# The gated delta rule on raw keys and queries, its triangular inverse from gathered left halves

## The chip, the cores and the metric

The kernel runs on one core of one Trainium2 chip. The metric is the device time of that core in microseconds (us), the median of the timed runs. Profiles come from one profiled execution, whose own time stands beside its span below.

## What is computed

Two blocks of two layers each run over 256 tokens of width 1024. The first block holds attention, a gated linear recurrence and memory attention. The second is a mixer (gated delta rule, retention, pooling, three gated branches) and a feed-forward part. The change lies in the gated delta rule alone, which runs twice, once in each layer of the second block. Cut to what matters, with 4 heads, head width 128 and chunks of 64 tokens:

```
q = l2_normalize(q); k = l2_normalize(k)          # x * rsqrt(sum(x*x) + 1e-6), per token and head
# gated_delta_rule(q, k, v, beta, g), everything per chunk of 64
q = q * dk**-0.5
G = cumsum(g); decay[i, j] = exp(G_i - G_j) for j <= i, else 0
k_beta = k * beta
m = strictly lower part of (k_beta k^T) * decay
sol = triangular_solve(m + eye, [v * beta, k_beta * exp(G)]);  u, w = sol
attn = (q k^T) * decay
q_dec = q * exp(G);  k_tail = k * exp(g_last - G)
# from chunk to chunk
v_new = u - w @ state
o = q_dec @ state + attn @ v_new
state = state * exp(g_last) + k_tail^T @ v_new
# afterwards: o * rsqrt(mean(o*o) + 1e-6) * gain
```

## The kernel before

All large products (projections, gates, branches, feed-forward) are done as three products of rounded float32 parts: a weight unit of 128x1024 is loaded into raw, ScalarE casts it to wh, VectorE takes the rest wl (class Stream), and mm3 (L537) or chan (L567) issues the products on TensorE into the PSUM tiles acc. This stream of weight products runs through the whole kernel.

Everything else is written as Python generators (tasks) that yield the tiles they wait for. While the program is being made, the class Order keeps a reckoned time of TensorE and of the other engines, with a fixed and a per-element cost for each instruction. After each few stream products poll() (L195) steps every task whose awaited tiles are reckoned ready by then (with HOP = 150 ns and SLACK = 200 ns, L151). So the program order on TensorE, which is the order in which it executes, mixes the task's small products into the stream at places that the reckoned times choose. The real engines then wait for each other by semaphores.

The delta rule is four tasks for each layer: dn_scalars (beta, g and the exponentials ex of the cumulated g), and for each tile t of 128 tokens (two chunks, 4 heads side by side) delta_tile (L1342), delta_side (L1468, spawned by it) and delta_scan (L1484). delta_tile of t = 1 starts when that of t = 0 has ended. All tiles are 128 partitions x 4 heads x 128 float32.

In delta_tile, T() transposes a tile head by head on TensorE into a PSUM tile mx, and mm() multiplies two tiles head by head into another. It transposes the convolved k and q to token rows (tiles cvk, cvq), takes their reciprocal norms (rms_heads, L432: a square on ScalarE, a sum and small steps on VectorE), makes kn and qn, transposes both back (knT, qnT), forms the decay E from psE, and M = -(beta) E * (kn kn^T) below the diagonal. kbg and ktail are kn scaled by rows.

The inverse of the unit triangular matrix is built over DN_LEVELS = (2, 4, 8, 16, 32, 64). Level 2 is a masked copy of M into W (tile dnT); its transpose is U. At each further level (the loop at L1429, n = 1 to 5) the right halves `new` of the blocks of U are replaced: a product of M with `new` into a PSUM tile, copied to X by ScalarE, a product of W with X, and a masked copy into U by VectorE; then, if n < 5, U is transposed to W for the next level. In the profile the first product reads dnU, dnM, the second dnX, dnT, and the transpose ident, dnU.

At the end the transposed v times beta and kbg are multiplied with U into u and one half of WQ. delta_side transposes the decayed query qd into the other half of WQ, and forms attnT from knT, qnT and E. delta_scan runs the recurrence over the chunks with the state st, adds the two parts of the output oi, normalises it by rms_heads and hands it on; it is transposed and used much later, in the branch "dn" behind the gates.

PSUM has 8 banks: 3 for acc, 5 for mx. SBUF tiles of these tasks come from a pool k2 of 24 buffers of 2 KB, longer ones from k4.

Of the kernel before, what the change touches and what calls it, by code (L numbers as in the profile page):

```python
# [14 lines left out]
ALU = mybir.AluOpType  # L15
# [3 lines left out]
P = 128  # L19
# [11 lines left out]
DN_LEVELS = (2, 4, 8, 16, 32, 64)  # L31
# [292 lines left out]
class Kernel:  # L324
# [15 lines left out]
    def big(self, pool, tag, shape, name, dt):  # L340
        self.uid += 1
        return pool.tile(list(shape), dt, tag=tag, name=f"{name}_{self.uid}")
# [86 lines left out]
            self.pe.transpose(tp[:, h, :], src[:, h * P : (h + 1) * P], self.ident)  # L429
        return tp  # L430

    def rms_heads(self, ps, scale=1.0 / P, eps=1e-6):  # L432

        junk = self.k2([P, 4, P], "junk")
        self.act.activation(junk, ps, AF.Square)
        yield junk
        ss = self.sm(4, "ss")
        self.dve.tensor_reduce(ss, junk, axis=AX.X, op=ALU.add)
        yield ss
        r = yield from self.rsqrt(ss, scale, eps, 4)  # L440
        return r

    def right(self, x, lev):
# [448 lines left out]
    def hgrn_z(self, lev, A, kx, qx):  # L892
# [3 lines left out]
        half = lev // 2  # L896
        E, Z = self.k2([P, 2, S], "hE"), self.k2([P, 2, S], "hZ")
        left, right = slice(0, half), slice(half, lev)
        Av, Ev, qv, kv, Zv = (x.rearrange("p h (b s) -> p (h b) s", s=lev) for x in (A, E, qx, kx, Z))
        n = 2 * S // lev  # L900
        if lev == 256:
            end = [A[:, :, 64 * c + 63 : 64 * c + 64] for c in range(3)]
            s01 = self.sm(2, "s01").unsqueeze(2)
            dve.tensor_tensor(s01, end[0], end[1], op=ALU.add)
            act.activation(E[:, :, 128:192], A[:, :, 128:192], AF.Exp)
            for c, b, scale in ((1, end[1], -1.0), (3, end[2], 1.0), (0, s01, -1.0)):
                cs = slice(64 * c, 64 * c + 64)
# [434 lines left out]
    def delta_tile(self, l, t, cv, sc, r):  # L1342

        act, dve, pe = self.act, self.dve, self.pe
        yield [f"dns{l}"] + [f"cv{l}{n}{j}" for n in "kqv" for j in range(2)] + ([f"dnt{l}0"] if t else [])
        yield [cv[n] for n in "kqv"]
        beta, g, ex = sc
        ts = slice(t * P, (t + 1) * P)
        hs = slice(4 * t, 4 * t + 4)
        bt = beta[:, t, :]  # L1350
        big = lambda tag: self.k2([P, 4, P], "dn" + tag)
        flat = lambda x: x.rearrange("p h d -> p (h d)")

        def T(c):
            tp = self.mx()
            for h in range(4):
                pe.transpose(tp[:, h, :], c[:, h, :], self.ident)
            return tp

        def mm(a, b):  # L1360
            ps = self.mx()
            for h in range(4):
                pe.matmul(ps[:, h, :], a[:, h, :], b[:, h, :], start=True, stop=True)
            return ps


        Bg = big("Bg")
        dve.tensor_tensor(Bg, self.dn_strict.unsqueeze(1).to_broadcast([P, 4, P]), self.bc(g[:, t, :]), op=ALU.mult)

        tk = T(cv["k"][:, :, ts])  # L1370
        tq = T(cv["q"][:, :, ts])
        yield [Bg, tk]
        psE = self.mx()
        for h in range(4):
            pe.matmul(psE[:, h, :], self.ident_bf, self.dn_neg, start=h == 0, stop=False, skip_group_check=True)
        pe.matmul(psE, self.dn_tri, Bg, start=False, stop=True, skip_group_check=True)
        rk = yield from self.rms_heads(tk, 1.0)
        E = big("E")
        act.activation(E, psE, AF.Exp)
        rq = yield from self.rms_heads(tq, 1.0)  # L1380
        kn = big("kn")
        dve.tensor_tensor(kn, tk, self.bc(rk), op=ALU.mult)
        yield kn
        tp = T(kn)
        bg, nb = self.sm(4, "bg"), self.sm(4, "nb")
        dve.tensor_tensor(bg, bt, ex[:, 0, hs], op=ALU.mult)
        dve.tensor_scalar(nb, bt, -1.0, None, op0=ALU.mult)
        kbg, ktail = big("kbg"), big("ktail")
        dve.tensor_tensor(kbg, kn, self.bc(bg), op=ALU.mult)
        dve.tensor_tensor(ktail, kn, self.bc(ex[:, 1, hs]), op=ALU.mult)  # L1390
        yield tp
        knT = big("knT")
        act.copy(knT, tp)

        qn = big("qn")
        dve.tensor_scalar(rq, rq, P**-0.5, None, op0=ALU.mult)
        dve.tensor_tensor(qn, tq, self.bc(rq), op=ALU.mult)

        yield knT
        psM = mm(knT, knT)  # L1400
        yield qn
        tp = T(qn)
        qd = big("qd")
        dve.tensor_tensor(qd, qn, self.bc(ex[:, 0, hs]), op=ALU.mult)
        nE = big("nE")
        dve.tensor_tensor(nE, E, self.bc(nb), op=ALU.mult)
        yield [psM, nE]
        M = big("M")
        dve.tensor_tensor(M, psM, nE, op=ALU.mult)

        W = big("T")
        mask = lambda n: self.dn_masks[:, n * P : (n + 1) * P].unsqueeze(1).to_broadcast([P, 4, P])
        act.copy(W, self.ident.unsqueeze(1).to_broadcast([P, 4, P]))
        yield [M, W]
        dve.copy_predicated(W, mask(0), M)
        yield tp
        qnT = big("qnT")
        act.copy(qnT, tp)
        yield W
        tp = T(W)  # L1420
        U = big("U")
        yield tp
        act.copy(U, tp)

        WQ = self.k4([P, 4, 2, P], "dnWQ")
        attnT = big("attnT")
        side = self.delta_side(T, mm, E, qnT, knT, qd, WQ, attnT)
        self.o.spawn(side, f"dnside{l}{t}")
        for n in range(1, 6):  # L1429
            lev = DN_LEVELS[n]  # L1430
            X = self.k2([P, 4, P // 2], "dnX")
            new = self.right(U, lev)
            yield [M, U]
            ps = self.mx((P, 4, P // 2))
            for h in range(4):
                pe.matmul(ps[:, h, :].rearrange("p (b s) -> p b s", s=lev // 2), M[:, h, :], new[:, h], start=True, stop=True)
            yield ps
            act.copy(X, ps)
            yield [X, W]
            ps = self.mx((P, 4, P // 2))  # L1440
            for h in range(4):
                pe.matmul(ps[:, h, :], W[:, h, :], X[:, h, :], start=True, stop=True)
            yield ps
            dve.copy_predicated(new, self.right(mask(n), lev), ps.rearrange("p h (b s) -> p h b s", s=lev // 2))
            if n < 5:
                yield U
                tp = T(U)
                yield tp
                W = big("T")
                act.copy(W, tp)  # L1450

        tp = T(cv["v"][:, :, ts])
        yield tp
        vb = big("vb")
        dve.tensor_tensor(vb, tp, self.bc(bt), op=ALU.mult)
        yield [U, kbg]
        ps = mm(kbg, U)
        yield ps
        for c in range(2):
            self.copy(WQ[:, :, c, c * 64 : (c + 1) * 64], ps[:, :, c * 64 : (c + 1) * 64])  # L1460
        yield vb
        u = big("u")
        ps = mm(U, vb)
        yield ps
        act.copy(u, ps)
        r[t] = u, WQ, attnT, ktail

    def delta_side(self, T, mm, E, qnT, knT, qd, WQ, attnT):  # L1468
        yield qd
        tp = T(qd)  # L1470
        yield tp
        for c in range(2):
            self.copy(WQ[:, :, c, (1 - c) * 64 : (2 - c) * 64], tp[:, :, c * 64 : (c + 1) * 64])
        yield [qnT, knT]
        ps = mm(qnT, knT)
        yield ps
        at = self.k2([P, 4, P], "dnat")
        self.dve.tensor_tensor(at, ps, E, op=ALU.mult)
        yield at
        tp = T(at)  # L1480
        yield tp
        self.copy(attnT, tp)

    def delta_scan(self, l, t, st, r, sc, on):  # L1484
        act, dve, pe = self.act, self.dve, self.pe
        yield [f"dnt{l}{t}", f"dnside{l}{t}"] + ([f"on{l}dn0"] if t else [])
        u, WQ, attnT, ktail = r[t]
        ex = sc[2]
        vn, oi = self.k2([P, 4, P], "vn"), self.k2([P, 4, P], "oi")
        for c in range(2):  # L1490
            q = slice(64 * c, 64 * c + 64)
# [4 lines left out]
            else:  # L1496
                yield [WQ, st]
                ps = self.mx()
# [8 lines left out]
            ps = self.mx()  # L1507
# [5 lines left out]
            else:  # L1513
                for h in range(4):
                    dve.scalar_tensor_tensor(st[:, h, :], st[:, h, :], ex[:, 2 + c, 4 * t + h : 4 * t + h + 1], ps[:, h, :],
                                             op0=ALU.mult, op1=ALU.add)
        yield [attnT, vn]
        ps = self.mx()
        for h in range(4):
            pe.matmul(ps[:, h, :], attnT[:, h, :], vn[:, h, :], start=True, stop=True)  # L1520
        yield [ps, oi]
        dve.tensor_tensor(oi, ps, oi, op=ALU.add)
        yield oi
        rr = yield from self.rms_heads(oi)
        on_ = self.k2([P, 4, P], "on")
        dve.tensor_tensor(on_, oi, self.bc(rr), op=ALU.mult)
        on["dn", t] = on_.rearrange("p h d -> p (h d)")
# [276 lines left out]
```

## Time and profile before

| | us |
|---|---|
| median of 3 runs | 1437.85 (1437.79 to 1439.17) |
| the profiled execution | 1441.07 |
| its span, first to last instruction | 1439.3 |
| TensorE busy | 1403.6 (98%) |
| VectorE busy | 1024.6 (71%) |
| ScalarE busy | 831.5 (58%) |
| GpSimd busy | 24.0 (2%) |

The first block takes about the first 460 us of the span; the mixers of the second block lie at about 460 to 752 and 948 to 1240 us, each followed by its feed-forward part. The delta rule lies at about 545 to 680 and 1033 to 1168 us. In the profile TensorE is PE, its loads of stationary tiles PEld, VectorE DVE, ScalarE ACT, GpSimd POOL. Almost all instructions are issued by helper lines (L108 for ACT, DVE and POOL, L134 for products, L142 for transposes), so groups are told apart by their tiles. The form of a product, as 128*64 128x64, is rows*columns of the stationary tile, then partitions x columns of the moving one. A float32 product is two instructions, a transpose or a product of rounded parts is one.

### The profile page before, as it was taken

Reading aid. Unit: us, or ns where it says so; the run is one execution under the profiler, and the core shown is the slowest. Engines: PE = TensorE matmul, PEld = TensorE weight load, DVE = VectorE, ACT = ScalarE, POOL = GpSimd, SP = SyncE. Lnnn points to the kernel's source line nnn. Section 1 sums busy time; section 2 is a strip of 40 time slices with the busy share of each in tenths; the row PEclk is TensorE's granted clock in tenths of the full one; section 3 lists DMA queues with packets and bytes.
Section 4 is the critical chain, followed back from the end, with each engine's and each line's share of the span. In section 5 each row is a group of like instructions: output and inputs, shape, how many; then the busy total and the mean of one; then the engine's idle time right before and its main releaser. Section 6 shows DMA issues by size and latency. Waiting matters only on the chain.

```text
span 1439.3 us, 24675 instructions
## 1 busy us (share of the span) xinstructions
PE 1403.6 (98%) x9772; PEld 1285.8 (89%) x9772; DVE 1024.6 (71%) x1684; ACT 831.5 (58%) x1396; POOL 24.0 (2%) x65
## 2 busy tenths in 40 slices
PE   6899999999998999999999999999999999999998
PEld 6778998888997899999988999979899999799997
DVE  5887778598777698585677656687976577765554
ACT  5875666586665476554655545556655456554553
POOL 6000000000000000000000000000000000000000
PEclk9999999999999999999999999999999999999999
DMA  8752455554256464253475666645543355566662
GB/s 273 173 163 75 132 206 177 185 164 118 60 188 228 126 186 126 90 162 97 156 235 166 186 188 189 215 136 156 153 135 109 105 154 204 184 190 190 184 183 88
DMA packets 156564, 231.41 MB, mean 161 GB/s; under 512 B 27168, under 2 KB 65696, under 8 KB 156448
## 3 DMA queue, kind: packets, MB, share of 16 engines
q1 hardware_dynamic: 156416, 229.84, 52.5%
q8 instruction: 76, 1.25, 0.4%
q14 instruction: 40, 0.33, 0.1%
q0 software_dynamic: 32, 0.00, 0.0%
HBM read 228.76 MB, written 1.05 MB: 160 GB/s over the span
## 4 chain that ended last, share of the span: by engine, by line
PE 76%; DMA 9%; DVE 8%; ACT 4%; issue 2%; SPq 0%; DVEq 0%; ACTq 0%
PE acc L134 53%; PE mx L134 19%; DVE wl L108 4%; PE mx L142 4%; DMA raw<-in_w_in 3%; DMA raw<-in_w_out 3%; ACT wh L108 3%; DMA raw<-in_ffn_up 1%; DMA raw<-in_w_mem_kv 1%; DVE aTl L108 1%; DMA raw<-in_ffn_down 0%; DVE x L108 0%; DMA gain<-in_norm_g 0%; ACT hE L108 0%; ACT junk L108 0%
## 5 line engine op out<-in xcount | busy, mean ns | idle before, releaser
L108 DVE TENSOR_TENSOR wl<-raw,wh 128x1024 fp32r<-128x1024 f32 x412 | 502.2, 1223 | 209.7 <-ACT wh L108 205.9
L108 ACT CAST wh<-raw 128x1024 fp32r<-128x1024 f32 x412 | 429.6, 1048 | 317.7 <-PE acc L134 148.7
L134 PE MATMUL acc<-aTh,wh 128*128 128x256 f32 x1792 | 514.1, 287 | 0.0
L134 PE MATMUL acc<-aTh,wl 128*128 128x256 f32 x1792 | 508.3, 284 | 0.6 <-DVE wl L108 0.6
L134 PE MATMUL acc<-aTl,wh 128*128 128x256 f32 x1792 | 507.6, 283 | 0.0
L134 PEld LDWEIGHTS acc<-aTh,wl 128*128 128x128 f32 x1792 | 343.5, 192 | 2.4 <-DVE wl L108 0.8
L134 PEld LDWEIGHTS acc<-aTh,wh 128*128 128x128 f32 x1792 | 343.4, 192 | 1.9 <-issue 0.5
L134 PEld LDWEIGHTS acc<-aTl,wh 128*128 128x128 f32 x1792 | 343.3, 192 | 0.0
L134 PE MATMUL acc<-wh,aTh 128*128 128x512 f32 x496 | 201.0, 406 | 6.0 <-ACT aTh L108 4.7
L134 PE MATMUL acc<-wh,aTl 128*128 128x512 f32 x496 | 195.4, 395 | 0.8 <-DVE aTl L108 0.8
L134 PE MATMUL acc<-wl,aTh 128*128 128x512 f32 x496 | 195.8, 395 | 0.0
L134 PEld LDWEIGHTS acc<-wh,aTh 128*128 128x128 f32 x496 | 94.4, 190 | 26.3 <-ACT aTh L108 5.8
L134 PEld LDWEIGHTS acc<-wh,aTl 128*128 128x128 f32 x496 | 93.9, 189 | 21.9 <-DVE aTl L108 2.3
L134 PE MATMUL mx<-wh,ff 128*128 128x512 f32 x352 | 111.6, 390 | 0.0
L134 PEld LDWEIGHTS acc<-wl,aTh 128*128 128x128 f32 x496 | 94.2, 190 | 18.4 <-issue 0.5
L134 PEld LDWEIGHTS mx<-wh,ff 128*128 128x128 f32 x352 | 66.2, 188 | 13.4
L108 ACT ACTIVATE sg<-sg 128x512 f32<-128x512 f32 x116 | 73.1, 630 | 1.9
L134 PE MATMUL mx<-wl,ff 128*128 128x512 f32 x176 | 68.7, 390 | 0.0
L108 ACT ACTIVATE sg<-zc 128x512 f32<-128x512 f32 x58 | 36.5, 628 | 22.8 <-DVE zc L108 22.8
L108 ACT ACTIVATE sig<-gz 128x512 f32<-128x512 f32 x24 | 15.2, 632 | 57.8 <-DVE gz L108 57.8
L134 PEld LDWEIGHTS mx<-wl,ff 128*128 128x128 f32 x176 | 33.1, 188 | 6.2
L108 DVE TENSOR_SCALAR zc<-acc 128x512 f32<-128x512 f32 x46 | 31.6, 686 | 9.5 <-PE acc L134 9.5
(311 smaller groups left out, 1593.0 us busy)
## 6 DMA issues: line engine op xcount, KB each, us to landing
raw<-in_w_in SPq DMA_DIRECT2D x200, 512.0 KB, 4.2
raw<-in_ffn_gate SPq DMA_DIRECT2D x44, 512.0 KB, 3.9
raw<-in_ffn_up SPq DMA_DIRECT2D x44, 512.0 KB, 4.6
raw<-in_ffn_down SPq DMA_DIRECT2D x44, 512.0 KB, 4.2
raw<-in_w_out SPq DMA_DIRECT2D x40, 512.0 KB, 3.8
raw<-in_w_mem_kv SPq DMA_DIRECT2D x16, 512.0 KB, 4.2
raw<-in_w_branch_pool SPq DMA_DIRECT2D x8, 512.0 KB, 3.7
raw<-in_w_branch_ret SPq DMA_DIRECT2D x8, 512.0 KB, 4.5
```

The costliest lines, as they stand in the source:

```text
L108: r = f(out, *args, **kw)
L134: self._ns.matmul(out, lhsT, rhs, **kw)
L142: self._ns.transpose(out, x, ident)
```

## The change

- q and k are no longer normalised as tiles. The k.k and q.k products, WQ and the recurrence take the raw convolved tiles cv, which are already transposed. The norms of k go into small row factors (br, nb, bg: 128x4), ktail takes the raw transposed k, those of q into rq, a factor of 128x2x4 that rms_heads of the output takes in (its new argument `after`); the factor exp(G) of the decayed query is applied to oi in delta_scan. Three of the transposes go (kn, qn, qd), with the tiles kn, qn, qd, knT and qnT; that of q moves into delta_side, with its rms_heads.
- At the levels n = 2 to 5 the left halves of M's columns are gathered by GpSimd into ML (128 x 4 x 64, four gathers for a tile, issued ahead of the loop), so that the first product has a stationary tile of 128 rows and 64 columns and X has 64 partitions. Before each of the transposes at n = 1 to 4 ScalarE gathers the left halves of U into UL (128 x 4 x 64); its transpose W has 64 partitions, and the second product contracts over 64. Level n = 1 keeps M, with W of 128 partitions.

```
-    def rms_heads(self, ps, scale=1.0 / P, eps=1e-6):
+    def rms_heads(self, ps, scale=1.0 / P, eps=1e-6, after=None):
...
+        if after is not None:
+            self.dve.tensor_tensor(ss, ss, after[:, 1, :], op=ALU.mult)
         yield ss
         r = yield from self.rsqrt(ss, scale, eps, 4)
+        if after is not None:
+            self.dve.tensor_tensor(r, r, after[:, 0, :], op=ALU.mult)
...
-        tk = T(cv["k"][:, :, ts])
-        tq = T(cv["q"][:, :, ts])
+        kT, qT = cv["k"][:, :, ts], cv["q"][:, :, ts]
+        psM = mm(kT, kT)
+        tk = T(kT)
...
         rk = yield from self.rms_heads(tk, 1.0)
+        br, nb, bg = self.sm(4, "br"), self.sm(4, "nb"), self.sm(4, "bg")
+        dve.tensor_tensor(br, bt, rk, op=ALU.mult)
+        dve.scalar_tensor_tensor(nb, br, -1.0, rk, op0=ALU.mult, op1=ALU.mult)
+        dve.scalar_tensor_tensor(bg, nb, -1.0, ex[:, 0, hs], op0=ALU.mult, op1=ALU.mult)
+        yield psE
         E = big("E")
         act.activation(E, psE, AF.Exp)
-        rq = yield from self.rms_heads(tq, 1.0)
-        kn = big("kn")
-        dve.tensor_tensor(kn, tk, self.bc(rk), op=ALU.mult)
-        yield kn
-        tp = T(kn)
...
-        kbg, ktail = big("kbg"), big("ktail")
-        dve.tensor_tensor(kbg, kn, self.bc(bg), op=ALU.mult)
-        dve.tensor_tensor(ktail, kn, self.bc(ex[:, 1, hs]), op=ALU.mult)
-        yield tp
-        knT = big("knT")
-        act.copy(knT, tp)
-
-        qn = big("qn")
-        dve.tensor_scalar(rq, rq, P**-0.5, None, op0=ALU.mult)
-        dve.tensor_tensor(qn, tq, self.bc(rq), op=ALU.mult)
-
-        yield knT
-        psM = mm(knT, knT)
-        yield qn
-        tp = T(qn)
-        qd = big("qd")
-        dve.tensor_tensor(qd, qn, self.bc(ex[:, 0, hs]), op=ALU.mult)
+        yield E
         nE = big("nE")
         dve.tensor_tensor(nE, E, self.bc(nb), op=ALU.mult)
         yield [psM, nE]
         M = big("M")
         dve.tensor_tensor(M, psM, nE, op=ALU.mult)
+        kbg, ktail = big("kbg"), big("ktail")
+        dve.tensor_tensor(kbg, tk, self.bc(bg), op=ALU.mult)
+        dve.tensor_tensor(ktail, tk, self.bc(ex[:, 1, hs]), op=ALU.mult)
+        del tk, psM, psE
...
-        yield tp
-        qnT = big("qnT")
-        act.copy(qnT, tp)
...
+        ML = [self.k2([P, 2, 4, P // 2], "dnML") for _ in range(2)]
+        ML = [None, None] + [x[:, i] for x in ML for i in range(2)]
+        for n in range(2, 6):
+            lev = DN_LEVELS[n]
+            self.o.gps.tensor_copy(ML[n].rearrange("p h (b s) -> p h b s", s=lev // 2),
+                                   M.rearrange("p h (b s) -> p h b s", s=lev)[..., : lev // 2])
         for n in range(1, 6):
             lev = DN_LEVELS[n]
-            X = self.k2([P, 4, P // 2], "dnX")
+            part = P if n == 1 else P // 2
+            X = self.k2([P, 4, P // 2], "dnX")[:part]
             new = self.right(U, lev)
-            yield [M, U]
-            ps = self.mx((P, 4, P // 2))
+            yield [M, U] + ([ML[n]] if n > 1 else [])
+            ps = self.mx((P, 4, P // 2))[:part]
             for h in range(4):
-                pe.matmul(ps[:, h, :].rearrange("p (b s) -> p b s", s=lev // 2), M[:, h, :], new[:, h], start=True, stop=True)
+                pe.matmul(ps[:, h, :].rearrange("p (b s) -> p b s", s=lev // 2), (M if n == 1 else ML[n])[:, h, :], new[:, h], start=True, stop=True)
...
             if n < 5:
+                UL = self.k2([P, 4, P // 2], "dnUL")
                 yield U
-                tp = T(U)
+                act.copy(UL.rearrange("p h (b s) -> p h b s", s=lev), U.rearrange("p h (b s) -> p h b s", s=2 * lev)[..., :lev])
+                yield UL
+                tp = self.mx()[: P // 2]
+                for h in range(4):
+                    pe.transpose(tp[:, h, :], UL[:, h, :], self.ident)
                 yield tp
-                W = big("T")
+                W = big("T")[: P // 2]
                 act.copy(W, tp)
...
-    def delta_side(self, T, mm, E, qnT, knT, qd, WQ, attnT):
-        yield qd
-        tp = T(qd)
-        yield tp
+    def delta_side(self, T, mm, E, qT, kT, rq, WQ, attnT):
         for c in range(2):
-            self.copy(WQ[:, :, c, (1 - c) * 64 : (2 - c) * 64], tp[:, :, c * 64 : (c + 1) * 64])
-        yield [qnT, knT]
-        ps = mm(qnT, knT)
+            self.copy(WQ[:, :, c, (1 - c) * 64 : (2 - c) * 64], qT[:, :, c * 64 : (c + 1) * 64])
+        ps = mm(qT, kT)
...
+        tq = T(qT)
+        yield tq
+        r = yield from self.rms_heads(tq, 1.0)
+        self.dve.tensor_scalar(rq[:, 0, :], r, P**-0.5, None, op0=ALU.mult)
+        self.dve.tensor_tensor(rq[:, 1, :], rq[:, 0, :], rq[:, 0, :], op=ALU.mult)
...
+        dve.tensor_tensor(oi, oi, self.bc(ex[:, 0, 4 * t : 4 * t + 4]), op=ALU.mult)
         yield [ps, oi]
         dve.tensor_tensor(oi, ps, oi, op=ALU.add)
         yield oi
-        rr = yield from self.rms_heads(oi)
+        rr = yield from self.rms_heads(oi, after=rq)
```

## Rows read from the trace of the kernel before

**Rows 1.** The page: engines' busy time and share; the cast of a weight unit

```profile
PE 1403.6 (98%) x9772; PEld 1285.8 (89%) x9772; DVE 1024.6 (71%) x1684; ACT 831.5 (58%) x1396; POOL 24.0 (2%) x65
...
L108 ACT CAST wh<-raw 128x1024 fp32r<-128x1024 f32 x412 | 429.6, 1048 | 317.7 <-PE acc L134 148.7
```

**Rows 2.** Stretches: length, busy of each engine (instructions), granted clock, DMA share, GB/s

```profile
500.00:740.00 240.00, 240.00 (x1882) 231.97 (x1882) 174.95 (x286) 141.22 (x220) 0.00 (x0) 1.00 0.48 147
755.50:762.40 6.90, 6.18 (x15) 4.84 (x16) 6.87 (x15) 3.95 (x11) 0.00 (x0) 0.51 0.59 168
```

**Rows 3.** PE's waits: engine, line, waited for: us in total, times, longest

```profile
PE mx L142 <- DVE xn L108: 16.9, 7, 10.4
```

**Rows 4.** Order of time on PE: start, length, operation, form; transposes of kn

```profile
619.93 0.28 PE L134 MATMUL acc<-aTh,wl 128*128 128x256 f32 x1
620.05 0.28 PE L134 MATMUL acc<-aTl,wh 128*128 128x256 f32 x1
620.17 0.60 PE L142 MATMUL mx<-ident,dnkn 128*128 128x128 f32 x4
...
620.72 0.28 PE L134 MATMUL acc<-aTh,wl 128*128 128x256 f32 x1
```

**Rows 5.** Order of time on PE around W.X of level n = 1

```profile
579.35 0.28 PE L134 MATMUL acc<-aTl,wh 128*128 128x256 f32 x1
579.47 1.00 PE L134 MATMUL mx<-dnX,dnT 128*128 128x64 f32 x8
...
580.48 0.28 PE L134 MATMUL acc<-aTh,wl 128*128 128x256 f32 x1
```

**Rows 6.** Order of time on PE: transpose of U, then M.new of n = 2

```profile
581.79 0.60 PE L142 MATMUL mx<-ident,dnU 128*128 128x128 f32 x4
582.23 1.00 PE L134 MATMUL mx<-dnU,dnM 128*128 128x64 f32 x8
```

**Rows 7.** Order of time on PE, first block: a group with 64 stationary columns

```profile
73.22 0.39 PE L134 MATMUL acc<-wl,aTh 128*128 128x512 f32 x1
73.44 0.39 PE L134 MATMUL acc<-wh,aTl 128*128 128x512 f32 x1
73.76 0.68 PE L134 MATMUL mx<-hZ 128*64 128x64 f32 x8
...
74.70 0.39 PE L134 MATMUL acc<-wl,aTh 128*128 128x512 f32 x1
```

**Rows 8.** Order of time on PE around a ktail product, 64 stationary rows

```profile
665.50 0.28 PE L134 MATMUL acc<-aTl,wh 128*128 128x256 f32 x1
665.70 1.16 PE L134 MATMUL mx<-vn,dnktail 64*128 64x128 f32 x8
...
667.01 0.28 PE L134 MATMUL acc<-aTh,wl 128*128 128x256 f32 x1
```

**Rows 9.** Loads of stationary tiles by form: busy us, mean ns, idle before

```profile
L134 PEld LDWEIGHTS mx<-hZ 128*128 128x128 f32 x144 | 18.1, 191 | 4.7 <-DVE hZ L108 3.9
...
L134 PEld LDWEIGHTS mx<-hZ 128*64 128x64 f32 x32 | 2.2, 137 | 1.4 <-issue 1.1 <-DVE hZ L108 0.4
```

**Rows 10.** Order of time on PE: two transposes with 8 moving columns

```profile
495.40 0.28 PE L142 MATMUL mx<-ident,ba 8*128 8x8 f32 x2
495.61 0.39 PE L134 MATMUL acc<-aTh,wh 128*128 128x256 f32 x1
```

**Rows 11.** Groups by form: the X copy, and the products on it

```profile
L108 ACT COPY dnX<-mx 128x256 f32<-128x256 f32 x20 | 7.4, 370 | 6.1 <-PE mx L134 6.1
...
L134 PE MATMUL mx<-dnX,dnT 128*128 128x64 f32 x160 | 20.5, 271 | 0.0
```

**Rows 12.** Order of time on DVE and PE: normalised output and its transposes

```profile
677.21 0.69 DVE L108 TENSOR_TENSOR on<-oi,r 128x512 f32<-128x512 f32 x1
...
695.30 1.04 PE L142 MATMUL mx<-ident,on 128*128 128x128 f32 x8
```

**Rows 13.** Groups by form on POOL: a cast of 512 columns

```profile
L108 POOL CAST dn_masks<-stage 128x512 uint8<-128x512 f32 x1 | 0.7, 712 | 9.3 <-DMA stage<-in_c_dn_masks 9.3
```

More of the change, by code (lines that the diff above doesn't have):

```diff
@@ L1377, in delta_tile @@
         rk = yield from self.rms_heads(tk, 1.0)
+        br, nb, bg = self.sm(4, "br"), self.sm(4, "nb"), self.sm(4, "bg")
[3 more added lines that the diff above has]
+        yield psE
         E = big("E")
         act.activation(E, psE, AF.Exp)
-        rq = yield from self.rms_heads(tq, 1.0)
-        kn = big("kn")
-        dve.tensor_tensor(kn, tk, self.bc(rk), op=ALU.mult)
-        yield kn
-        tp = T(kn)
-        bg, nb = self.sm(4, "bg"), self.sm(4, "nb")
-        dve.tensor_tensor(bg, bt, ex[:, 0, hs], op=ALU.mult)
-        dve.tensor_scalar(nb, bt, -1.0, None, op0=ALU.mult)
-        kbg, ktail = big("kbg"), big("ktail")
-        dve.tensor_tensor(kbg, kn, self.bc(bg), op=ALU.mult)
-        dve.tensor_tensor(ktail, kn, self.bc(ex[:, 1, hs]), op=ALU.mult)
-        yield tp
-        knT = big("knT")
-        act.copy(knT, tp)
-        qn = big("qn")
-        dve.tensor_scalar(rq, rq, P**-0.5, None, op0=ALU.mult)
-        dve.tensor_tensor(qn, tq, self.bc(rq), op=ALU.mult)
-        yield knT
-        psM = mm(knT, knT)
-        yield qn
-        tp = T(qn)
-        qd = big("qd")
-        dve.tensor_tensor(qd, qn, self.bc(ex[:, 0, hs]), op=ALU.mult)
+        yield E
         nE = big("nE")
@@ L1426, in delta_tile @@
         attnT = big("attnT")
-        side = self.delta_side(T, mm, E, qnT, knT, qd, WQ, attnT)
-        self.o.spawn(side, f"dnside{l}{t}")
+        rq = self.t(self.p_lay, [P, 2, 4], "dnrq")
+        self.o.spawn(self.delta_side(T, mm, E, qT, kT, rq, WQ, attnT), f"dnside{l}{t}")
+        ML = [self.k2([P, 2, 4, P // 2], "dnML") for _ in range(2)]
[4 more added lines that the diff above has]
+                                   M.rearrange("p h (b s) -> p h b s", s=lev)[..., : lev // 2])
         for n in range(1, 6):
             lev = DN_LEVELS[n]
-            X = self.k2([P, 4, P // 2], "dnX")
+            part = P if n == 1 else P // 2
+            X = self.k2([P, 4, P // 2], "dnX")[:part]
             new = self.right(U, lev)
-            yield [M, U]
-            ps = self.mx((P, 4, P // 2))
+            yield [M, U] + ([ML[n]] if n > 1 else [])
+            ps = self.mx((P, 4, P // 2))[:part]
             for h in range(4):
-                pe.matmul(ps[:, h, :].rearrange("p (b s) -> p b s", s=lev // 2), M[:, h, :], new[:, h], start=True, stop=True)
+                pe.matmul(ps[:, h, :].rearrange("p (b s) -> p b s", s=lev // 2), (M if n == 1 else ML[n])[:, h, :], new[:, h], start=True, stop=True)
             yield ps
@@ L1454, in delta_tile @@
         vb = big("vb")
-        dve.tensor_tensor(vb, tp, self.bc(bt), op=ALU.mult)
+        dve.tensor_tensor(vb, tp, self.bc(br), op=ALU.mult)
         yield [U, kbg]
@@ L1465, in delta_tile @@
         act.copy(u, ps)
-        r[t] = u, WQ, attnT, ktail
-    def delta_side(self, T, mm, E, qnT, knT, qd, WQ, attnT):
-        yield qd
-        tp = T(qd)
-        yield tp
+        r[t] = u, WQ, attnT, ktail, rq
+    def delta_side(self, T, mm, E, qT, kT, rq, WQ, attnT):
         for c in range(2):
-            self.copy(WQ[:, :, c, (1 - c) * 64 : (2 - c) * 64], tp[:, :, c * 64 : (c + 1) * 64])
-        yield [qnT, knT]
-        ps = mm(qnT, knT)
+            self.copy(WQ[:, :, c, (1 - c) * 64 : (2 - c) * 64], qT[:, :, c * 64 : (c + 1) * 64])
+        ps = mm(qT, kT)
         yield ps
@@ L1486, in delta_scan @@
         yield [f"dnt{l}{t}", f"dnside{l}{t}"] + ([f"on{l}dn0"] if t else [])
-        u, WQ, attnT, ktail = r[t]
+        u, WQ, attnT, ktail, rq = r[t]
         ex = sc[2]
```

## The prediction

> **What bounds the kernel now.** I read the page first: TensorE (PE) is busy for 98% of the span [rows 1]. A busy PE need not be a fast one, so I then took the busy time by stretch. In the stretch of the first mixer in which the changed code runs, PE is busy for all of its 240 us at full clock [rows 2]. The list of PE's waits confirms it: the longest entry is 16.9 us for the normalised activations at the starts of phases [rows 3], and none is for a tile of the delta rule. So around the delta rule no engine and no transfer sets the pace: PE works through a stream of weight products (tiles acc) without a gap, and the delta rule's groups are cut into that stream. What such a group costs is what it pushes the stream back, and this can be read exactly from the order of time: from the start of the last stream product before the group to the start of the second one behind it, less two normal pitches. A pitch is 0.12 us for a stream product of 256 columns (619.93 to 620.05 in [rows 4]) and 0.227 for one of 512 (73.22 to 73.44 in [rows 7]). Every length in VectorE, ScalarE or GpSimd is cover as long as PE finds its operand ready.
>
> **The prices.** A group of four transposes: 620.05 to 620.72, less 0.24, is 0.43 us [rows 4]. A group of four float32 products on a 128x128 stationary tile (two instructions each): 579.35 to 580.48, less 0.24, is 0.89 [rows 5]; it has 64 moving columns, so the load of the stationary columns paces it. Four such products with 128 rows and 64 stationary columns: 73.44 to 74.70, less 0.45, is 0.81 [rows 7]. Four with 64 rows and 128 columns: 665.50 to 667.01, less 0.24, is 1.27 [rows 8]. These last two are the core of the case. Half the columns save next to nothing and half the rows cost more than the whole, because at such a group the stream breaks off: the first product starts 0.32 behind the last of the stream instead of 0.227 in the one [rows 7], 0.20 instead of 0.12 in the other [rows 8].
>
> **The change part by part**, for 4 tiles (2 layers by 2) with 4 gathered levels each, so 16 of each kind a level.
>
> (a) Normalised k, normalised q and decayed q are no longer transposed. That is 3 groups of four a tile: 12 x 0.43 = 5.2 us less. The transposes of raw k and raw q stay (q's moves into delta_side), and the k.k and q.k products keep their shape, so 0.43 and 0.89 each are paid as before.
>
> (b) W.X at four levels contracts over 64 rows. The nearest group is the ktail product [rows 8], with the same stationary shape and type in the same stream; its 128 moving columns instead of 64 do not matter where the load paces. 16 x (1.27 - 0.89) = 6.1 us more. The bounds are 6.1 and, if the half height did not break the stream, 0 (the old price); a gain is rival 5. I take 6.1, the row of that very shape.
>
> (c) M.new at four levels has 64 stationary columns and 64 moving ones, the shape of the group of the first block in [rows 7]: 16 x (0.81 - 0.89) = 1.3 us less. Bounded by 0 and, if the break of the stream were free, by half the old price: 16 x 0.45 = 7.1 less. I take the row of the same shape.
>
> (d) The transposes of U have 64 stationary columns. No row shows a float32 transpose of 64 columns, so I bound it. A transpose now has a pitch of 0.11: 0.44 for four (581.79 to 582.23 in [rows 6]). The two small ones with only 8 moving columns also take 0.21 together [rows 10], so the load paces a transpose. A load of 64 columns takes 137 ns where one of 128 takes 191 [rows 9], 54 ns less. That makes 4 x 0.054 = 0.22 a group and 16 x 0.22 = 3.5 us less. The other end is 0, if the transpose uses the whole array whatever its width. I take 3.5, since the load paces and it is the load that is halved; this is the least certain term.
>
> (e) The rest I cost at nothing, with its cover. Four gathers of M a tile go to GpSimd, idle there (POOL 0.00 in [rows 2]); a cast of 512 columns took 0.71 us [rows 13], so four take under 2.9, and between the second product of level 1 and the first of level 2 alone lie 2.8 us (579.47 to 582.23 in [rows 5, 6]). If that cover were gone, four first gathers would cost under 3 us in all. The gather of U puts one more ScalarE copy, of the size of the X copy (370 ns [rows 11]), between the mask copy and the transpose at 16 places. PE does not stand still meanwhile: the helper that orders the instructions puts stream products there until it reckons the copy done. On ScalarE the weight splits queue behind it, 16 x 0.37 = 6 us, against the eight copies of the transposed kn and qn that go, and PE waits for neither. The factor exp(G) moves to a multiplication of oi in delta_scan, 0.69 us on VectorE; the normalised output is ready at 677.9 and is transposed at 695.3 [rows 12], so 17 us hide it and the small multiplications of rms_heads. The chain up to M becomes shorter by one rms_heads and one transpose, which PE does not wait for. Three PSUM buffers of the five (raw k, psM, psE) are held until M; before, it was raw k, raw q and psE.
>
> The sum: -5.2 + 6.1 - 1.3 - 3.5 = -3.9 us. Against the profiled execution (1441.07 us, of which the span is 1439.3) this is 0.27%; applied to the median of the runs shown, 1437.85, it gives **1434.0 us**. The profiled run stands 3.2 above that median, a difference of executions that I leave as it is.
>
> **Weighed against the skill.** [Rows 8] show the half-height stationary tile as the dearer one. The Trainium skill (TensorEngine Tiling (Array Packing), Theoretical Speedup) lists a small dimension of 64 or less as worth up to 2x. By that, W.X would fall from 0.89 to 0.45 a group, 7.1 us less instead of 6.1 more, and the sum would be -17.1. That speed-up is for independent tiles side by side; all four heads here lie on partitions 0 to 63.
>
> **The rivals.**
> 1. The forecast, 1434.0.
> 2. Term (d) is nothing: a float32 transpose of 64 columns costs what one of 128 does. For it: no row shows one. Against it: the load paces [rows 9, 10]. Then the sum is -0.4 and the time 1437.5, no difference. The Trainium skill (TensorEngine Tiling (Array Packing), Gotcha 2: Feature Incompatibilities) says that column tiling excludes transpose mode for float32 input, so the transpose would run on the full array; whether its load is then still half as long, it does not say.
> 3. The gather of U is exposed. If ScalarE has a weight split ahead of it that the ordering did not reckon with, PE, which takes instructions in order, stands at the transpose for the copy and a split. Price: the copy's 0.37 and 1.05 us of split (the cast into wh in [rows 1]). At half of the 16 places that is 8 x 1.42 = 11.4 us, so +7.5 and 1445.3; it is slower than before from an exposure of 0.25 us a place (3.9 / 16), and measurably so from 0.43. Against it: no wait of PE for the delta rule's copies stands in the list, and PE's idle time before the products on the X copy, made in the same way at 20 places, is 0.0 [rows 11].
> 4. PE's saving is swallowed because the weights set the pace. For it: each weight unit still needs its transfer, its cast and its rest. Against: the transfers take a share of 0.48 and PE has no gap in this stretch [rows 2]. Then 1437.9.
> 5. The half-height tile is the faster one: W.X at half of 0.89, so -5.2 - 7.1 - 1.3 - 3.5 = -17.1 and 1420.8. Against it stand [rows 8].
>
> **How the numbers follow.** Chances: forecast 0.54, rival 2 0.24, rival 3 0.12, rival 4 0.06, rival 5 0.04. A measurement of this kernel tells about 0.2%, 2.9 us, from no change. The forecast is only 1 us beyond that bound, and 0.10 of its 0.54 I count as no difference. Faster: 0.44 + 0.04 = 0.48. Same: 0.10 + 0.24 + 0.06 = 0.40. Slower: 0.12. One thing moves by itself: from 755.5 to 762.4 the granted clock is 0.51, so 1.2 GHz, after PE's waits at the change of phase [rows 2]. Half of those 6.9 us, 3.4, can go, or come at another change of phase. So the range runs from 1434.0 - 3.4 = 1430.6 to a little beyond rival 2 with part of rival 3, 1440.0.
>
> **What would show it right or wrong.** In the order of time of the changed kernel: (a) groups of transposes of dnkn, dnqn and dnqd are gone; (b) products of the new tile of W with 64*128 at about 1.27 by the same reckoning; (c) products with 128*64, at about 0.8 behind a transpose; (d) transposes of dnUL with a pitch near 0.055, which rival 2 would show at 0.11. PE stays without gaps between the phases; if idle time before L142 for dnUL appears among its waits, rival 3 holds. The prediction is wrong if a 64-row product with 64 moving columns costs something else than one with 128, if the break is smaller directly behind a transpose, or if new gaps stand at the changes of phase.

## The result: slower by 1%, and where the time stands in the profile after

The changed kernel takes 1453.68 us (median; 1452.42 to 1455.37) against 1437.82 of the kernel before it was timed with. The ratio is 1.0104 [1.009, 1.0119], or 15.9 us more, where 3.9 us less was forecast. Its profiled execution took 1453.89 us, with a span of 1452.1.

The page (busy us of PE; share; instructions), the list of PE's waits and the table by stretches (length, PE, PEld, DVE, ACT, POOL, granted clock, DMA share, GB/s) of the changed kernel:

```profile
PE 1402.2 (97%) x9724; PEld 1278.1 (88%) x9724; DVE 1022.7 (70%) x1690; ACT 836.1 (58%) x1406; POOL 32.1 (2%) x81
```

```profile
PE mx L142 <- DVE xn L108: 32.8, 7, 9.9
```

```profile
500.00:740.00 240.00, 240.00 (x1860) 228.18 (x1859) 174.67 (x289) 143.79 (x225) 4.32 (x8) 1.00 0.50 149
750.00:760.00 10.00, 0.90 (x4) 0.40 (x3) 8.42 (x17) 6.23 (x14) 0.00 (x0) 0.66 0.74 222
```

PE is busy 1.4 us less than in [rows 1], but its wait for the normalised activations xn went from 16.9 us [rows 3] to 32.8. About 10 us of either lie at the very start of the kernel (10.4 and 9.9); what grew are the waits at two places, from 1.35 and 0.34 us to 9.29 and 9.13. The spans of these two executions differ by 12.8 us, so the growth of the wait, 15.9, is more than the whole difference: PE's other idle time is 1.7 us less, and its busy time 1.4. That 15.9 is also the difference of the medians is chance, since the profiled execution of the kernel before stood 3.2 above its median. The delta rule's own stretch is as it was in [rows 2]: PE without idle time, at full clock. The new time lies behind it, where the second block's mixers hand over to their feed-forward part, near 750 and near 1244 us. The order of time there, of ScalarE, VectorE and TensorE (start, length, idle time before and its releaser), in the changed kernel; the last line is the second handoff:

```profile
742.78 0.60 ACT L108 ACTIVATE junk<-acc 128x512 bf16<-128x512 f32 x1
...
747.20 1.05 ACT L108 CAST wh<-raw 128x1024 fp32r<-128x1024 f32 x1 [3.73 <-DMA raw<-in_ffn_up]
748.15 0.30 ACT L108 ACTIVATE y<-ss,b 128x1 f32<-128x1 f32 x1
...
749.29 0.20 ACT L108 ACTIVATE y<-y 128x1 f32<-128x1 f32 x1
...
748.29 2.36 DVE L108 TENSOR_TENSOR wl<-raw,wh 128x1024 fp32r<-128x1024 f32 x2 [3.34 <-ACT wh L108]
750.57 0.21 DVE L108 SCALAR_TENSOR_TENSOR w<-y,v 128x1 f32<-128x1 f32 x1
...
751.89 0.15 DVE L108 SCALAR_TENSOR_TENSOR r<-w,z 128x1 f32<-128x1 f32 x1
...
759.39 1.41 DVE L108 SCALAR_TENSOR_TENSOR xn<-x,r,gain 128x512 f32<-128x512 f32 x2
...
750.51 0.39 PE L134 MATMUL mx<-wh,aTl 128*128 128x512 f32 x1
760.19 1.97 PE L142 MATMUL mx<-ident,xn 128*128 128x128 f32 x8 [9.29 <-DVE xn L108]
...
1253.83 1.97 PE L142 MATMUL mx<-ident,xn 128*128 128x128 f32 x8 [9.13 <-DVE xn L108]
```

The same place in the kernel before:

```profile
744.88 0.59 ACT L108 ACTIVATE junk<-acc 128x512 bf16<-128x512 f32 x1
...
746.41 0.29 ACT L108 ACTIVATE y<-ss,b 128x1 f32<-128x1 f32 x1 [0.85 <-DVE c L108]
746.74 0.20 ACT L108 ACTIVATE y<-y 128x1 f32<-128x1 f32 x1
746.85 1.98 ACT L108 CAST wh<-raw 128x1024 fp32r<-128x1024 f32 x2
...
747.21 0.22 DVE L108 SCALAR_TENSOR_TENSOR w<-y,v 128x1 f32<-128x1 f32 x1
...
753.21 1.41 DVE L108 SCALAR_TENSOR_TENSOR xn<-x,r,gain 128x512 f32<-128x512 f32 x2
...
752.28 0.39 PE L134 MATMUL mx<-wh,aTl 128*128 128x512 f32 x1
754.02 1.32 PE L142 MATMUL mx<-ident,xn 128*128 128x128 f32 x8 [1.35 <-DVE xn L108]
...
1241.24 1.32 PE L142 MATMUL mx<-ident,xn 128*128 128x128 f32 x8 [0.34 <-DVE xn L108]
```

At this place post_norm squares the mixer's output (junk<-acc), takes y as Ln and Exp on ScalarE, w, r and x on VectorE, and the next norm turns x into xn. Before, y follows 0.9 us behind the squares and the weight casts come after it. In the changed kernel a cast stands between the squares and y. It waits 3.73 us for a transfer of in_ffn_up that has not landed, and since ScalarE executes in order, y waits too (in this trace all 1309 instructions that the program gives ScalarE, and all 1690 of VectorE, ran in the program's order). On VectorE the subtraction wl<-raw,wh of the same unit stands ahead of w. From the last product before the gap to the first transpose, less a pitch of 0.227 us, PE loses 760.19 - 750.51 - 0.23 = 9.45 us, where it lost 754.02 - 752.28 - 0.23 = 1.51 before. At the second handoff the same reckoning gives 9.29 against 0.49. In the gap and behind it the granted clock is down (0.66 over 750 to 760), which is 1.2 of 2.4 GHz for part of it: the eight transposes behind the gap take 1.97 us instead of 1.32.

Which cast it is can be read from the two programs: the one of unit 204, the first of the feed-forward's in_ffn_up (350 in the second layer). Its transfer is issued behind those of 202 and 203, in both kernels. Stream._can_place gives a unit one of 6 buffers w, and if none is reckoned free, for some units one of 2 spare buffers k4. Before, 204 was placed in w and 201 in k4. In the changed kernel Order reckons the delta rule shorter, and 201 gets w and 204 the spare. A buffer w comes free only when an earlier unit has been used, which kept the cast of 204 back; a spare is free at once, so in the finished instruction order the cast comes first. In the Python code it is issued after post_norm's y in both. The same goes for 350 and 347; in the layer's second output projection 196 and 342 changed places with 192 and 338.

The delta rule itself, in the changed kernel: a transpose of UL with the product on ML behind it, and a product W.X over 64 rows:

```profile
578.94 0.28 PE L134 MATMUL acc<-aTl,wh 128*128 128x256 f32 x1
579.06 0.60 PE L142 MATMUL mx<-ident,dnUL 128*64 128x128 f32 x4
579.59 0.68 PE L134 MATMUL mx<-dnU,dnML 128*64 128x64 f32 x8
580.20 0.38 PE L134 MATMUL acc<-aTh,wh 128*128 128x256 f32 x1
580.42 0.28 PE L134 MATMUL acc<-aTh,wl 128*128 128x256 f32 x1
...
581.61 0.28 PE L134 MATMUL acc<-aTl,wh 128*128 128x256 f32 x1
581.82 1.10 PE L134 MATMUL mx<-dnX,dnT 64*128 64x64 f32 x8
582.85 0.39 PE L134 MATMUL acc<-aTh,wh 128*128 128x256 f32 x1
583.07 0.28 PE L134 MATMUL acc<-aTh,wl 128*128 128x256 f32 x1
```

By the prediction's reckoning the pair costs 580.42 - 578.94 - 0.24 = 1.24 us, of which 0.53 pass between the start of the first transpose and that of the first product. Before, it cost 1.33, the median of 14 such pairs; their order is that of [rows 6]. W.X costs 583.07 - 581.61 - 0.24 = 1.22 (0.89 in [rows 5]).

### The profile page after: what moved, and what is told of

Same layout as the page of the kernel before. It is cut to its first block, busy times and chain, and to the rows that moved or that the text cites. A ratio compares the mean times of both kernels' runs of the same rounds, so it can differ in the third digit from the quotient of the medians.

```text
span 1452.1 us, 24636 instructions
## 1 busy us (share of the span) xinstructions
PE 1402.2 (97%) x9724; PEld 1278.1 (88%) x9724; DVE 1022.7 (70%) x1690; ACT 836.1 (58%) x1406; POOL 32.1 (2%) x81
## 3 DMA queue, kind: packets, MB, share of 16 engines
HBM read 228.76 MB, written 1.05 MB: 158 GB/s over the span
## 4 chain that ended last, share of the span: by engine, by line
PE 75%; DMA 9%; DVE 8%; ACT 5%; issue 3%; SPq 0%; DVEq 0%; ACTq 0%
PE acc L134 52%; PE mx L134 19%; DVE wl L108 4%; PE mx L142 4%; ACT wh L108 3%; DMA raw<-in_w_out 3%; DMA raw<-in_w_in 3%; DMA raw<-in_ffn_gate 1%; DMA raw<-in_ffn_up 1%; DMA raw<-in_w_mem_kv 1%; ACT sg L108 0%; SPq L363 0%; DMA gain<-in_norm_g 0%; DVE zc L108 0%; DVE x L108 0%
## 5 line engine op out<-in xcount | busy, mean ns | idle before, releaser
L142 PE MATMUL mx<-ident,xn 128*128 128x128 f32 x128 | 21.5, 314 | 32.8 <-DVE xn L108 32.8
L142 PEld LDWEIGHTS mx<-ident,xn 128*128 128x128 f32 x128 | 17.3, 162 | 37.0 <-DVE xn L108 33.3
```

Source lines behind the costliest of these rows:

```text
L142: self._ns.transpose(out, x, ident)
```

## The experiments

Two theories stood against each other. One: the loss is the order on the in-order queues at the two handoffs, set by the buffers, and the delta rule itself is a small gain. The other: the changed delta rule makes it, by later ends, its gathers or the clock.

### Buffers of before with the change, buffers of the change without it

```
-        if self.used["w"] < self.SLOTS:
-            return "w"
-        if self.units[self.n_h][2] and self.used["k4"] < self.SPARE:
-            return "k4"
-        return None
+        k4 = [52, 59, 112, 119, 121, 127, 192, 199, 201, 207, 260, 261, 268, 269, 338, 345, 347, 353, 406, 407]
+        if self.n_h in k4:
+            return "k4" if self.used["k4"] < self.SPARE else None
+        return "w" if self.used["w"] < self.SLOTS else None
```

That is the list of the kernel before, put into the changed kernel. For the second run the list of the changed kernel (196, 204, 342, 350 for 192, 201, 338, 347) is put into the kernel before.

> The whole change, with one thing put back: the weight units are put into the same buffers (k4 spares or w) as in the kernel before, so unit 204 of layer 1 and unit 350 of layer 2 wait for a w buffer again instead of taking a k4 spare, and their casts stand behind post_norm's Ln and Exp on ScalarE. Theory (the loss is ScalarE's order at the two handoffs from mixer to feed-forward): the gaps of PE near 750 and 1244 us go from 9.5 and 9.3 us back to about 1.5 and 0.5, the longest waits of mx on xn from 32.8 us to about 17, and the time is 1437.8 less about 1 to 2, so 1435.5 to 1437.5 us. Rival (the gaps come of the changed delta rule itself, by its later ends, its GpSimd gathers or a longer fall of the clock): it stays within 3 us of 1453.7 us.

> The kernel before, its delta rule untouched; only the buffers of the weight units are those of the changed kernel (units 204 and 350 in k4 spares, 201 and 347 in w, and of the second output projection's units 196 and 342 in k4 in place of 192 and 338). Theory (slots and ScalarE's order): about 16 us lost, 1452 to 1456 us, with gaps of about 9 us at both handoffs. Rival (the changed delta rule itself): within 2 us of 1437.8 us.

Measured: 1435.50 us, ratio to before 0.9987 [0.9978, 0.9996], and 1455.49 us, ratio 1.0128 [1.0108, 1.0147]. The list of waits of the first and then of the second:

```profile
PE mx L142 <- DVE xn L108: 15.4, 7, 9.9
```

```profile
PE mx L142 <- DVE xn L108: 33.1, 7, 10.5
```

The stretch behind the handoff in the first:

```profile
750.00:760.00 10.00, 8.08 (x37) 5.93 (x36) 9.49 (x20) 6.04 (x14) 0.00 (x0) 1.00 0.68 225
```

In the instruction list of the second run the cast of 204 stands ahead of y, as in the changed kernel, with nothing but the list of buffers changed. The placement alone makes the loss in a kernel whose delta rule is untouched, and taking it back removes the loss from the changed one. The granted clock stays at 1.00 in this stretch, where PE's gap is 1.0 us; in the kernel before, behind a gap of 1.5, it was at 0.51 from 755.5 on [rows 2]. The second theory falls.

### One layer only

The list of before for layer 1, that of the change for layer 2 (342 and 350).

> The whole change with the buffers of the weight units as before in layer 1 (unit 204 in w) and as in the changed kernel in layer 2 (unit 350 in a k4 spare). Theory (each handoff loses on its own, through the cast that stands ahead of post_norm's Ln): half of the loss, PE's gap near 750 us about 1 us and that near 1240 us about 9 us, time 1435.5 + 9 = 1444.5 us (1443 to 1446.5). Rival (the two handoffs are bound together, or another of the moved units makes the loss): near 1436 or near 1453.7 us.

Measured: 1446.26 us (1442.82 to 1447.08), ratio 1.0052 [1.0038, 1.0066], half of the loss.

```profile
PE mx L142 <- DVE xn L108: 24.2, 7, 10.1
```

The wait lies half way too. PE's gap is 1.6 us at the first handoff and 8.6 at the second: each loses by itself.

### The two halves of the change

Raw keys and queries with the loop of the inverse as before, and the gathered loop with normalised k and q as before. In both, the buffers come out as in the kernel before, without a list.

> The change's first part alone: keys and queries raw, three groups of transposes per tile less, levels of the inverse over full matrices as before. Slots come out as before by themselves. Theory by step (a) of the prediction, 12 groups of 0.43 us less: 1432.6 us (1431.5 to 1434). Rival (the saving is hidden behind a wait of PE elsewhere): 1437 to 1438 us. Rival (raw keys lengthen the chain ahead of the first level, since M waits for the norms of tk): slower than 1438 us, with new waits of PE in the delta stage.

> The change's second part alone: the gathered left halves at four of five levels, keys and queries normalised and transposed as before. Slots come out as before by themselves. By the prediction's own sizes (W.X 16 x +0.38, M.new 16 x -0.08, T(UL) -3.5): 1439.1 us. By the sizes read from the changed kernel's trace (T(UL) costs what T(U) cost, W.X 16 x +0.33, ML.new about -1.4 in all): 1441.7 us. Rival (half tile is worth its half): 1426 us.

> Raw keys and queries alone once more, beside the two others, for a direct comparison: 1431.6 us, ratio 0.9961 to the kernel before.

Measured: raw alone 1431.57 us, ratio 0.9961 [0.9945, 0.9976], and once more 1432.57, 0.9955 [0.9939, 0.9970]. Gathered alone 1441.05, ratio 1.0025 [1.0014, 1.0037]. The first half gains 5.4 us as forecast; the second costs 4.1 and is no gain at all. Together -1.2, which is within noise what the change gives with the buffers of before (1435.50 - 1436.93 = -1.4). So the parts add up, and raw keys alone is the fastest of all kernels run here. Neither half moves the buffers by itself; that the two together do is bad luck, which neither half foretells.

### Where in the queues: the casts on GpSimd

```
-        self.o.act.copy(h[:, :w], self.raw[i][:, :w])
+        if i in (204, 350):
+            self.o.gps.tensor_copy(h[:, :w], self.raw[i][:, :w])
+        else:
+            self.o.act.copy(h[:, :w], self.raw[i][:, :w])
```

> The changed kernel with its own buffers, units 204 and 350 in k4 spares; only their two casts run on GpSimd instead of ScalarE, so that post_norm's Ln and Exp follow its squares on ScalarE at once, while the same transfers land in the same order. Theory (it is the place in ScalarE's queue): most of the loss is gone, gaps of PE under 2.5 us at both handoffs, time 1436 to 1439 us (casts of 205, 206 and 207 still stand ahead of the second norm's Ln there). Rival (the transfer or the buffer is what PE waits for, not the queue): the gaps stay at 9 us and the time at 1453 us; GpSimd's cast being slow could make the unit itself late, and then acc waits for wh or wl of unit 204.

Measured: 1454.57 us, ratio 1.0114 [1.0099, 1.0128]. I was wrong: nothing came back. Order of time:

```profile
743.84 0.20 ACT L108 ACTIVATE y<-y 128x1 f32<-128x1 f32 x1
...
747.11 1.05 POOL L108 CAST wh<-raw 128x1024 fp32r<-128x1024 f32 x1 [127.22 <-DMA raw<-in_ffn_up]
...
748.18 1.23 DVE L108 TENSOR_TENSOR wl<-raw,wh 128x1024 fp32r<-128x1024 f32 x1 [3.86 <-POOL wh L108]
749.33 0.21 DVE L108 SCALAR_TENSOR_TENSOR w<-y,v 128x1 f32<-128x1 f32 x1
```

y is there at 744.0, 5.5 us earlier than in the changed kernel, but w starts at 749.33: VectorE stands at the subtraction of the same unit, which is also ahead of the norm in its order. My theory had named one queue where there are two. So both steps went to GpSimd (the subtraction likewise, for the same units), once with the whole change and once with raw keys alone:

> The changed kernel with its own buffers (204 and 350 in k4 spares); the cast and the subtraction (wl<-raw,wh) of these two units both run on GpSimd. The run with the casts alone moved kept its gap: there y was ready at 743.84 us, and VectorE, which has the unit's subtraction ahead of post_norm's w, waited for the unit until 748.18. Theory (the unit stands ahead of the norm on both in-order queues, ScalarE's and VectorE's): with both steps gone from them the gaps of PE near 750 and 1243 us fall to about 1 us and the time to 1434 to 1437 us. Rival (the gap comes with the buffer or the transfer, wherever the two steps run): 1450 us or more. Rival (GpSimd's subtraction is so slow that the unit comes late): the gap moves to acc<-wh or acc<-wl behind the handoff, 1438 to 1448 us.

> Raw keys and queries alone, buffers as they come out (204 and 350 in w, as in the kernel before), and both steps of units 204 and 350 on GpSimd: one cast of 1.0 us and one subtraction of 1.2 us less ahead of xn at either handoff. Theory (xn is late there by these): up to 1.5 us less than raw alone, that is 1430 to 1431.6 us. Rival (GpSimd makes the units late, or the rest of the chain is as long): 1431.6 us or a little over.

Measured: 1450.82 us, ratio 1.0078 [1.0061, 1.0095], and 1437.60, 0.9991 [0.9978, 1.0003], which is 5.0 over raw keys alone (1432.57 beside it). Both missed their forecasts: the first lies where its first rival put it, the second is slower than raw keys alone. Order of time of the first of the two:

```profile
750.10 2.15 POOL L108 CAST wh<-raw 128x1024 fp32r<-128x1024 f32 x1 [127.62 <-DMA raw<-in_ffn_up]
752.33 2.37 POOL L108 TENSOR_TENSOR wl<-raw,wh 128x1024 fp32r<-128x1024 f32 x1
...
752.35 2.36 DVE L108 SCALAR_TENSOR_TENSOR r<-w,z 128x1 f32<-128x1 f32 x1
...
755.56 1.32 PE L142 MATMUL mx<-ident,xn 128*128 128x128 f32 x8 [2.05 <-DVE xn L108]
761.82 0.79 PE L134 MATMUL acc<-wh,aTh 128*128 128x512 f32 x1 [4.94 <-ACT aTh L108]
...
758.71 1.04 ACT L108 CAST wh<-raw 128x1024 fp32r<-128x1024 f32 x1 [7.76 <-DMA raw<-in_ffn_up]
...
761.18 0.59 ACT L108 CAST aTh<-mx 128x512 fp32r<-128x512 f32 x1
```

The wait for xn did fall, from 9.29 us to 2.05, as the corrected theory says. But the gap came back behind it. The subtraction on GpSimd ends at 754.70 and only then frees the unit's raw buffer, one of three. The next transfer of in_ffn_up lands late, and its cast, which waits 7.76 us for it, stands on ScalarE ahead of the cast aTh that PE needs. It is the same fault one unit further on. This run bears the theory out for xn, but not the forecast of the time.

### The order alone

The buffers of the change stay, and so do the engines. Only a write of one column from post_norm's y (rms_rstd keeps them in a list) into the unit's wh goes ahead of the cast:

```
+        if i in (204, 350):
+            self.o.act.copy(h[:, :1], self.kb.ys[-1])
         self.o.act.copy(h[:, :w], self.raw[i][:, :w])
```

> The changed kernel with its own buffers (204 and 350 in k4 spares) and both steps on ScalarE and VectorE as in it; only, one element per partition of wh is first written from post_norm's y (128x1 on ScalarE, overwritten by the cast), so that the cast of unit 204 or 350 cannot stand ahead of post_norm's Ln and Exp. It still stands ahead of the squares of x. Theory (order on the two in-order queues, not the buffer): by the changed kernel's times y comes at 743.5 us as the squares end, x at 744.9, the cast waits for its transfer till 747.2, then squares, casts of 202 and 203 and three subtractions follow, and xn starts at 753.2 in place of 759.4: the gap shrinks by 6 us to 3 or 4 us at either handoff, time 1453.7 - 12 = 1441.5 us (1440 to 1444). Rival (the spare buffer as such, wherever its unit stands in the queues): gaps of 9 us, 1453 us. Rival (no wait at all stays, as with the buffers of before): 1435.5 us.

Measured: 1440.54 us (1436.97 to 1442.57), ratio 1.0013 [1.0003, 1.0023]. Order of time in its profiled execution, the shortest of its twelve:

```profile
743.36 0.30 ACT L108 ACTIVATE y<-ss,b 128x1 f32<-128x1 f32 x1
...
745.53 2.00 ACT L108 CAST wh<-raw 128x1024 fp32r<-128x1024 f32 x2 [1.42 <-DMA raw<-in_ffn_up]
...
751.39 1.41 DVE L108 SCALAR_TENSOR_TENSOR xn<-x,r,gain 128x512 f32<-128x512 f32 x2
...
752.20 1.32 PE L142 MATMUL mx<-ident,xn 128*128 128x128 f32 x8 [1.44 <-DVE xn L108]
```

This is 1.2 us over the kernel before timed beside it (1439.39), where the changed kernel was 15.9 over it and the one with the buffers of before 1.4 under. So with the same buffers 14.7 us are back, a little more than expected. The spare buffer as such does not make the loss; the order that it leads to does. The remaining 2.6 us fit the cast that still stands, and waits (1.42 us here), ahead of the squares of x, but I did not try that place by itself.

### The price of a product over 64 rows

In the changed kernel with the buffers of before, and in raw keys alone, the 16 products W.X of n = 2 to 5 are issued twice:

```
-            for h in range(4):
+            for h in [0, 1, 2, 3] * (2 if n > 1 else 1):
                 pe.matmul(ps[:, h, :], W[:, h, :], X[:, h, :], start=True, stop=True)
```

> The whole change with the buffers of before, and each of the 16 products W.X over 64 rows is issued twice over (8 more instructions in the same group). It prices such an instruction without its neighbours. If the price lies at the two ends of a 64-row group (the trace of the changed kernel has pitches of 112 ns inside it, longer ones of about 0.2 us at either end): 128 instructions x 112 ns = +14.3 us over 1435.5, so 1449.8 us (1448 to 1451.5). If each 64-row instruction costs its share of the group's price (1.22 us for 8): +19.6 us, 1455 us.

> Raw keys and queries alone, and the same 16 products W.X, here over all 128 rows, issued twice. Price of 8 more instructions inside a group at 111 ns: +14.2 us over 1431.6, so 1445.8 us (1444 to 1447.5), that is the same as over 64 rows if a 64-row product differs at its ends only. Rival (a full-height instruction is cheaper inside a group too, as 0.89 us for 8 against 1.22): more than 4 us less is added here than in the run over 64 rows.

Measured: 1451.83 us, ratio 1.0103 [1.0087, 1.0118], and 1448.49, ratio 1.0075 [1.006, 1.009]. Set against the kernel before timed beside it (1438.68 here, 1436.93 for the single products), each median rose by nearly the same: 13.15 + 1.43 = 14.6 us and 9.81 + 5.36 = 15.2, near the 14.3 and 14.2 expected. The trace of the first, then of the second:

```profile
582.97 0.28 PE L134 MATMUL acc<-aTl,wh 128*128 128x256 f32 x1
583.18 2.00 PE L134 MATMUL mx<-dnX,dnT 64*128 64x64 f32 x16
...
585.33 0.28 PE L134 MATMUL acc<-aTh,wl 128*128 128x256 f32 x1
```

```profile
579.24 0.28 PE L134 MATMUL acc<-aTl,wh 128*128 128x256 f32 x1
579.36 1.90 PE L134 MATMUL mx<-dnX,dnT 128*128 128x64 f32 x16
...
581.27 0.28 PE L134 MATMUL acc<-aTh,wl 128*128 128x256 f32 x1
```

16 instructions cost 585.33 - 582.97 - 0.24 = 2.12 us, so the 8 added ones 0.90, or 112 ns each. Over all 128 rows the same reckoning gives 581.27 - 579.24 - 0.24 = 1.79, less 0.89 = 0.90. A product over 64 rows costs no more than a full one inside its group; the 0.33 us lie at the group's two ends.

## Why the prediction was wrong

The forecast was 1434.0 in a range of 1430.6 to 1440.0, with 12% on slower. It is wrong in its sign. Step by step:

- **What bounds the kernel:** right for the delta rule's stretch, and the method of pricing by start times holds: with the groups as they turned out, the halves come to -5.2 and +3.9 us, and -5.4 and +4.1 were measured. But the argument stopped at the stretch's end.
- **(a)** Three groups of transposes gone, -5.2: right. Raw alone measures -5.4 and -6.6 us.
- **(b)** W.X, +6.1: 16 x (1.22 - 0.89) = +5.3. Right in mechanism, a little large. With 128 moving columns the group of [rows 8] has a break of the same kind at either end.
- **(c)** The product on 64 stationary columns, -1.3: right. The pair with the transpose costs 1.24 instead of 1.33. The four transposes span 0.60 us as before, so 0.44 is still their price; the 0.09 more up to the first product is the break ahead of it, which its row [rows 7] has as well. So the product costs 1.24 - 0.44 = 0.80, and 16 x (0.80 - 0.89) = -1.4.
- **(d)** The transposes of UL, -3.5: wrong, and rival 2 had it. Each group costs 0.44 as before: 0. The step that failed is that the load paces a transpose. Loads by form (busy us, mean ns), the changed kernel and then the kernel before:

```profile
L142 PEld LDWEIGHTS mx<-ident,dnUL 128*64 128x64 f32 x64 | 6.9, 111 | 0.0
```

```profile
L142 PEld LDWEIGHTS mx<-ident,dnU 128*128 128x128 f32 x64 | 7.1, 140 | 0.3
```

The load did become shorter by 29 ns, yet four transposes still span 0.60 us, as in [rows 6]. The reading of [rows 10] that the step rested on was wrong too: in that trace the second small transpose starts 0.08 us behind the first (495.48 after 495.40), and the rest of the 0.21 is the end of the group. The transposes of UL keep their 128 moving columns; whether these pace them was not taken apart. The Trainium skill (TensorEngine Tiling (Array Packing), Gotcha 2: Feature Incompatibilities), which rival 2 cited, says that column tiling excludes transpose mode for float32 input. The unchanged span agrees with that, though no run shows how the array was set.

- **The sum** of (a) to (d) is then -5.2 + 5.3 - 1.4 + 0 = -1.3 us, and with the buffers of before -1.4 was measured (1435.50 us). Against the forecast's -3.9 this is the smaller error.
- **(e)** "The rest I cost at nothing" is the step that turned the sign. It went through instructions, copies and PSUM buffers of the delta rule, but not through what its reckoned times set elsewhere: which of the later weight units takes a spare buffer, and by that where its cast and subtraction stand on ScalarE and VectorE. The text named "new gaps at the changes of phase" as a way to be wrong and gave it neither a rival nor a price. It costs about 17 us: 15.9 over the kernel before with the new places, 1.4 under it with the old. The prediction read the 16.9 us of [rows 3] as waits at the starts of phases, but 10.4 of them lie at the start of the kernel; at the two handoffs PE waited only 1.35 and 0.34 us for xn. Small as they are, these waits were the sign: xn already came last there, so whatever delays it goes straight into PE's time.
- **Rival 3** was close in kind, a weight split ahead of a short instruction on ScalarE, but looked for it at the copies of U, where no wait is listed. Rivals 4 and 5 did not occur: raw keys show their gain in the time, and W.X became dearer.

## What to carry to other kernels

Where the instruction order comes from reckoned times, a shorter stage can move buffers and with them the order of engines far behind it, so compare the order around each phase change first. If a stage gained and the kernel lost, look on each in-order queue for an instruction that waits for a transfer ahead of a short one on the critical chain, and remember that the unit has a step on more than one queue. Test the halves of a change apart: here one half alone (0.9955 to 0.9961) beats both kernels.

## What the runs showed of the hardware that I had not expected

Work moved to an idle GpSimd slows VectorE. While GpSimd ran its subtraction (752.33 to 754.70), r<-w,z of 128x1 on VectorE took 2.36 us, ending with it, where it took 0.15 in the changed kernel (751.89). GpSimd's cast took 2.15 us beside a subtraction on VectorE and 1.05 with VectorE idle. The Trainium skill (SBUF — State Buffer, Who interferes with whom) says that an instruction of VectorE with two SBUF inputs contends with one of GpSimd that reads SBUF; these rows agree. The same shows in raw keys with both steps on GpSimd (1437.60 against 1432.57 us): w<-y,v took 2.02 us beside GpSimd's subtraction, where it took 0.22 in raw keys alone, and PE waited 1.92 and 2.05 us for xn at the two handoffs instead of 0.34 and 0.33. That is 3.3 of the 5.0 us; the rest was not taken apart.

A group over 64 rows is dear only at its ends: 0.33 us in all against a full group, and no difference inside.
